# Host-side layouts in place of on-chip transposes, GpSimd pow for one norm, and an early weight load in an 8-core hybrid decoder trunk

## The chip, the cores and the metric

The kernel is one launch on all 8 cores of a Trainium2 chip (two dies, cores 0 to 3 and 4 to 7). No core talks to another: each does one prompt sequence and one share of the samples with the same weights. The metric is the device time of the slowest core in microseconds.

A program on all eight cores has two states here. In the fast one all cores agree within some 1%. In the slow one the cores of one die, sometimes of both, show a lower granted TensorE clock and the run takes some 2 to 14 per cent longer. Every comparison below is of fast runs, or of the cores of an undisturbed die, unless it says otherwise. The experiments ran on several chips; the fast runs of before beside them took 4237 to 4245 us, and one 4263, so a difference of a few us between two of them means little.

## The reference, cut to what matters

```
h = x                                           # (rows, 1024); 2048 prompt rows and 128 sample rows per core
for each of 4 layers:
    z = rmsnorm(h, g_mix) @ w_in                # columns: group A, then u, v (group B), then c_in (group C)
    A: y_a = gate_b * dwconv3(gate_c * xa)      # history hist_a: 2 rows per sample
    B: y_b = gelu(u) * (W_s @ layernorm(gelu(v)) + b_s)       # causal within chunks of 128 rows
    C: y_c = silu(layernorm(dwconv31(glu(c_in))))             # history hist_c: 30 rows per sample
    h += concat(rmsnorm(y_a), rmsnorm(y_b), rmsnorm(y_c)) @ w_out
    h += (silu(f @ w_gate) * (f @ w_up)) @ w_down             # f = rmsnorm(h)
    h += sigmoid(rmsnorm(h) @ w_ple_gate) * (p[i] @ w_ple_proj)
return rmsnorm(h), the new conv histories, the new v rows
```

Matrices are bf16 on the engine, x, p, the histories and all outputs are f32 in memory.

Of the kernel before, what the change touches and what calls it, by code (L numbers as in the profile page):

```python
# [7 lines left out]
F32 = mybir.dt.float32  # L8
# [5 lines left out]
DEPTH = 4  # L14
# [13 lines left out]
NV = NVL * DEPTH + 8  # L28
ENGS = ("pe", "act", "dve", "pool", "sp")
# [57 lines left out]
def build_program():  # L87
# [8 lines left out]
    xin = din("xin", [2176, D])  # L96
    pin = din("pin", [DEPTH, 2176, 256])
    sa = din("sa", [DEPTH, 32, 384])
    sc = din("sc", [DEPTH, 480, 256])
# [14 lines left out]
    y_o = dout("y", [2176, D])  # L114
    nap_o = dout("nap", [DEPTH, 2, 384])
    nas_o = dout("nas", [DEPTH, 32, 384])
    ncp_o = dout("ncp", [DEPTH, 30, 256])
    ncs_o = dout("ncs", [DEPTH, 480, 256])
# [5 lines left out]
    with es:  # L124
# [18 lines left out]
        STG = sb("STG", [128, 2, 1024], F32)  # L143
# [15 lines left out]
        NEGH = sb("NEGH", [128, 1], F32)  # L159
        PSTG = sb("PSTG", [128, 4, 256], F32)  # L160
# [5 lines left out]
        semnames = list(ENGS) + [f"d{i}" for i in range(NDS)] + [f"w{i}" for i in range(NS)]  # L166
        SEM = {n: es.enter_context(nc.semaphore("s_" + n)) for n in semnames}

        st = {"bank": 0, "sbank": 0, "ds": 0, "stg": 0, "sq": 0, "rb": 0, "tmp": 0, "pstg": 0, "pumpk": 3}
# [216 lines left out]
        def transpose_in(src_rows_ap, nrows, ncolchunks, evac):  # L386
            pass

# [3 lines left out]

        for hf in range(2):
# [18 lines left out]
            for (col0, row0, _) in tiles:  # L412
                si = ring("stg", 2)
                bi = blk_of_col(col0)
                for hh_ in range(2):
                    dma(STG[:, si, hh_ * 512:(hh_ + 1) * 512], xin[row0:row0 + 128, hh_ * 512:(hh_ + 1) * 512],
                        writes=[("STG", si, hh_)], fence=[("STG", si)])
                for half8 in range(2):
                    bank = newbank()
                    for k4 in range(4):  # L420
                        kc = half8 * 4 + k4
                        S.op("pe", lambda e, kc=kc, k4=k4, bank=bank, si=si: e.transpose(
                            PS[:, bank, k4 * 128:(k4 + 1) * 128], STG[:, si, kc * 128:(kc + 1) * 128], IDF[:]),
                            reads=[("STG", si, half8), ("STG", si), ("IDF",)], writes=[("ps", bank)], inc=(1 if k4 == 3 else 0))
                    S.op("act" if half8 == 0 else "dve",
                         (lambda e, bank=bank, half8=half8, col0=col0: e.activation(
                             H[:, half8 * 4:half8 * 4 + 4, col0:col0 + 128],
                             PS[:, bank, :].rearrange("p (k c) -> p k c", k=4), AF.Copy)) if half8 == 0 else
                         (lambda e, bank=bank, half8=half8, col0=col0: e.tensor_copy(
                             H[:, half8 * 4:half8 * 4 + 4, col0:col0 + 128],  # L430
                             PS[:, bank, :].rearrange("p (k c) -> p k c", k=4))),
                         writes=[("ps", bank)] + [("H", half8 * 4 + k, bi) for k in range(4)])

            for l in range(DEPTH):
# [15 lines left out]
                if hf == 0:  # L450
                    for j in range(2):
                        S.op("pool", lambda e, j=j: e.memset(GB[:, j, 0:30], 0.0), writes=[("Gh", j)])
                    si = ring("stg", 2)
                    dma(STG[0:32, si, 0:384], sa[l], writes=[("STG", si)])
                    bank = newbank()
                    for j in range(3):
                        S.op("pe", lambda e, j=j, bank=bank, si=si: e.transpose(
                            PS[:, bank, j * 32:(j + 1) * 32], STG[0:32, si, j * 128:(j + 1) * 128], IDF[0:32, 0:32]),
                            reads=[("STG", si), ("IDF",)], writes=[("ps", bank)], inc=(1 if j == 2 else 0))
                    S.op("dve", lambda e, bank=bank: e.tensor_copy(  # L460
                        XAH[:, :, :], PS[:, bank, 0:96].rearrange("p (j c) -> p j c", j=3)),
                        writes=[("ps", bank), ("XAH",)])
                    for rt in range(4):
                        nr = 128 if rt < 3 else 96
                        si = ring("stg", 2)
                        dma(STG[0:nr, si, 0:256], sc[l, rt * 128:rt * 128 + nr, :], writes=[("STG", si)])
                        bank = newbank()
                        for j in range(2):
                            S.op("pe", lambda e, j=j, bank=bank, si=si, nr=nr: e.transpose(
                                PS[:, bank, j * 128:j * 128 + nr], STG[0:nr, si, j * 128:(j + 1) * 128],  # L470
                                IDF[0:nr, 0:nr]),
                                reads=[("STG", si), ("IDF",)], writes=[("ps", bank)], inc=(1 if j == 1 else 0))
                        S.op("dve", lambda e, bank=bank, rt=rt, nr=nr: e.tensor_copy(
                            GFS[:, :, rt * 128:rt * 128 + nr],
                            PS[:, bank, 0:256].rearrange("p (j c) -> p j c", j=2)[:, :, 0:nr]),
                            writes=[("ps", bank)] + [("GFS", j) for j in range(2)])
                    for j in range(2):
                        S.op("pool", lambda e, j=j: e.tensor_copy(GB[:, j, GS0:GS0 + 480], GFS[:, j, 0:480]),
                             reads=[("GFS", j)], writes=[("Gsh", j)])
                else:  # L480
                    for j in range(2):
                        S.op("pool", lambda e, l=l, j=j: e.tensor_copy(GB[:, j, 0:30], CARG[:, l, j, :]),
                             reads=[("CARG", l)], writes=[("Gh", j)])

                pt_h = {}
                pload, ptrans = [], []
                for ti_, (col0, row0, _) in enumerate(tiles):
                    pi = ti_ % 4

                    def pld(pi=pi, row0=row0, l=l):  # L490
                        dma(PSTG[:, pi, :], pin[l, row0:row0 + 128, :], writes=[("PSTG", pi)])
                    pload.append(pld)

                    def pstep(pi=pi, col0=col0):
                        bank = newbank()
                        for j in range(2):
                            S.op("pe", lambda e, j=j, bank=bank, pi=pi: e.transpose(
                                PS[:, bank, j * 128:(j + 1) * 128], PSTG[:, pi, j * 128:(j + 1) * 128], IDF[:]),
                                reads=[("PSTG", pi), ("IDF",)], writes=[("ps", bank)], inc=(1 if j == 1 else 0))
                        S.op("act", lambda e, bank=bank, col0=col0: e.activation(  # L500
                            PT[:, :, col0:col0 + 128], PS[:, bank, 0:256].rearrange("p (j c) -> p j c", j=2), AF.Copy),
                            writes=[("ps", bank), ("PT", col0 // 128)])
                    ptrans.append(pstep)
                for ti_ in range(min(4, ntile)):
                    bg_add([pload[ti_]])
                for ti_ in range(ntile):
                    pt_h[ti_] = bg_add([ptrans[ti_]])
                    if ti_ + 4 < ntile:
                        bg_add([pload[ti_ + 4]])
# [27 lines left out]
                for tbi, tb in enumerate(range(0, ntile, 3)):  # L537
                    batch = list(range(tb, min(tb + 3, ntile)))
                    for ti_ in batch:
# [13 lines left out]
                             writes=[("BST", gi)])  # L553
                        pump(st["pumpk"])
                    if tbi + 1 < nblk:
                        u_block(tbi + 1)
                    for ti_ in batch:
                        col0, row0, kind = tiles[ti_]
                        gi = ti_ % 3
                        S.op("act", lambda e, gi=gi: e.activation(BST[:, gi, 7:8], BST[:, gi, 7:8], AF.Ln, bias=EPSC[:, 0:1]),  # L560
                             reads=[("EPSC",)], writes=[("BST", gi)])
                        S.op("act", lambda e, gi=gi: e.activation(BST[:, gi, 7:8], BST[:, gi, 7:8], AF.Exp, scale=-0.5),
                             writes=[("BST", gi)])
# [46 lines left out]
                if hf == 0:  # L610
# [3 lines left out]
                    for rt in range(4):  # L614
                        nr = 128 if rt < 3 else 96
                        bank = newbank()
                        for j in range(2):
                            S.op("pe", lambda e, j=j, bank=bank, rt=rt, nr=nr: e.transpose(
                                PS[0:nr, bank, j * 128:(j + 1) * 128],
# [455 lines left out]
```

## The kernel before: what the change and the argument touch

On the chip everything lies transposed: features on the 128 partitions, tokens along the free axis. Memory has tokens as rows, so the kernel before turns every input and output block with a TensorE transpose against an identity (IDF), by way of PSUM and a staging buffer. A core works through its tokens in two halves. The first half has blocks of 512, 512 and 128 columns (the last are the samples), the second 384, 384 and 256; each half runs all four layers. In a layer the order is: U and V (group B's two inputs), group C's two inputs, conv C by diagonal matrices DG, W_s, group A, w_out, the SwiGLU pair, and P, the gated p stage, which ends the layer.

Loading x, one 128-row tile at a time through two STG buffers (S.op puts an operation into an engine's queue; reads, writes and fences give the waits):

```python
for (col0, row0, _) in tiles:
    si = ring("stg", 2)
    for hh_ in range(2):
        dma(STG[:, si, hh_*512:(hh_+1)*512], xin[row0:row0+128, hh_*512:(hh_+1)*512], ...)   # SyncE's queue
    for half8 in range(2):
        bank = newbank()
        for k4 in range(4):
            S.op("pe", transpose(PS[:, bank, k4*128:(k4+1)*128], STG[:, si, kc*128:(kc+1)*128], IDF))
        S.op("act" if half8 == 0 else "dve", copy(H[:, half8*4:half8*4+4, col0:col0+128], PS[:, bank, :]))
```

The histories and the state outputs go the same way through the same two STG buffers, p through four PSTG buffers with its copies on ScalarE, y through STG again. (cut)

The layer norm of V, a batch of three 128-row tiles at a time (in short form):

```python
for ti_ in batch:                                # V matmuls, Gelu into one of three VG buffers, statistics
    mmgroup(PS[:, bk, 0:384], ...); S.op("act", VG[gi] = Gelu(PS[bk]))
    S.op("dve", bn_stats); S.op("dve", bn_aggr)
if tbi + 1 < nblk: u_block(tbi + 1)              # the next block of U: matmuls and three Gelus
for ti_ in batch:
    S.op("act", BST = Ln(var + EPS)); S.op("act", BST = Exp(-0.5 * BST))
    S.op("dve", VG = (VG - mean) * rstd)
    S.op("pool", VG = VG * gain); S.op("pool", VN = VG + bias)
```

Weights come through a ring of five slots by GpSimd's DMA queue; `try_load()` fills the slots that are free, and before it is first called when the first matmul group is built. W_s is loaded into VG and masked into MP by GpSimd, so the first V Gelu of a layer has to wait for MP.

## Time and profile before

| kernel before, five runs | us |
|---|---|
| median | 4734.76 |
| the one fast run (the profiled one) | 4257.77 |
| the four slow runs | 4687.31 to 4795.66 |

In profile lines PE is TensorE, PEld its weight loads, ACT ScalarE, DVE VectorE, POOL GpSimd and SP SyncE; a "q" behind the name marks the engine's instruction queue, where DMAs are issued. L310 is line 310 of the kernel that ran, PS is PSUM (where matmuls write), SLOT a weight slot. A DMA has landed when its data is in place. Read the profile in this order: the cores (is the run fast?), the busy shares (PE is highest), the slices (where does PE dip?), then what ends the waits in the dips. The lines stand in the prediction below.

### The profile page before, as it was taken

To read this page: it belongs to the slowest core of one execution; us is meant where nothing else is said; L and a number is where in the kernel's file an instruction comes from. 1 tells how busy PE (TensorE), PEld (TensorE's weight loads), DVE (VectorE), ACT (ScalarE), POOL (GpSimd) and SP (SyncE) were. 2 spreads that over 40 slices of the span, in tenths; PEclk is the share of its full clock that TensorE was granted. 3 is DMA by queue.
4 is the path that set the end of the run, shared out by engine and by line. 5 is a ranking of instruction groups with operands and counts; after the bars stand their busy time and mean duration, and the time that the engine had idled before them with its cause. 6 is when DMAs were issued, how large, how long until landed. Compare 5 with 4: busy or idle time off the path is not lost.

```text
span 4256.2 us, 67802 instructions; the slowest of 8 cores (4208.0 to 4256.2 us)
## 1 busy us (share of the span) xinstructions
PE 3737.4 (88%) x23068; PEld 2146.4 (50%) x23068; DVE 1861.0 (44%) x3543; ACT 1427.8 (34%) x2817; POOL 514.7 (12%) x642
## 2 busy tenths in 40 slices
PE   6899979799887999779996789987998789987997
PEld 3444534355443554435543556654665556654665
DVE  3452263622545325453253452455326353455325
ACT  3331143511435214342144341254215341344214
POOL 2100013000030000300000200020001200020010
PEclk9988999899998999989996999998999899998998
DMA  5333444244351442513435335441445335441542
GB/s 107 50 53 52 64 60 56 40 66 63 50 74 29 66 72 44 80 17 60 70 53 130 45 57 80 70 62 37 75 65 73 45 58 79 70 62 23 76 74 64
DMA packets 363568, 263.00 MB, mean 62 GB/s; under 512 B 117076, under 2 KB 330084, under 8 KB 363236
## 3 DMA queue, kind: packets, MB, share of 16 engines
q0 software_dynamic: 333696, 216.03, 36.8%
q1 hardware_dynamic: 29540, 42.65, 3.2%
q8 instruction: 196, 3.21, 0.3%
q14 instruction: 136, 1.11, 0.1%
HBM read 461.86 MB, written 12.78 MB: 112 GB/s over the span
## 4 chain that ended last, share of the span: by engine, by line
PE 69%; DVE 9%; ACT 8%; DMA 6%; issue 5%; POOL 1%; DVEq 0%; SPq 0%; ACTq 0%; POOLq 0%
PE PS L310 65%; DVE NRM L373 4%; PE PS L362 3%; DMA SLOT<-w_down 2%; DMA SLOT<-w_ple_gate 1%; DVE TMP L750 1%; ACT L316 1%; ACT L699 1%; ACT L560 1%; POOL VG L567 1%; DVE XA L735 1%; DMA STG<-xin 1%; ACT SQ L354 1%; ACT RB L316 1%; POOL VN L577 1%
## 5 line engine op out<-in xcount | busy, mean ns | idle before, releaser
L310 PE MATMUL PS<-NRM,SLOT 128*128 128x512 bf16 (+3 forms) x14592 | 2434.9, 326 | 96.1 <-DVE NRM L373 18.9
L310 PEld LDWEIGHTS PS<-NRM,SLOT 128*128 128x128 bf16 x14592 | 1359.8, 100 | 1088.2 <-issue 264.9
L883 ACT ACTIVATE TMP<-PS 128x512 f32<-128x512 f32 (+3 forms) x528 | 249.3, 473 | 1453.4 <-PE PS L310 1411.1
L885 DVE TENSOR_TENSOR Y<-TMP,PS 128x512 bf16<-128x512 f32 (+3 forms) x528 | 281.0, 532 | 1004.5 <-PE PS L310 879.5
L310 PE MATMUL PS<-Y,SLOT 128*128 128x512 bf16 (+3 forms) x4224 | 670.7, 319 | 12.5 <-DMA SLOT<-w_down 12.2
L310 PEld LDWEIGHTS PS<-Y,SLOT 128*128 128x128 bf16 x4224 | 385.4, 98 | 289.6 <-issue 41.1
L901 DVE TENSOR_TENSOR H<-H,PS 128x512 f32<-128x512 f32 (+3 forms) x576 | 300.2, 531 | 355.4 <-PE PS L310 338.5
L362 PE MATMUL PS<-SQ,ONES 128*128 128x512 bf16 (+3 forms) x816 | 213.8, 345 | 131.5 <-ACT SQ L354 128.3
L354 ACT ACTIVATE SQ<-H 128x512 bf16<-128x512 f32 (+3 forms) x624 | 274.5, 496 | 158.5 <-PE PS L362 101.9
L373 DVE SCALAR_TENSOR_TENSOR NRM<-H,VEC,RB 128x512 bf16<-128x512 f32 (+3 forms) x576 | 305.8, 603 | 42.6 <-ACT RB L318 42.2
L310 PE MATMUL PS<-GB,DG 128*128 128x512 bf16 (+3 forms) x1488 | 233.1, 317 | 0.0
L272 POOL DMA_DIRECT2D SLOT<-w_gate x72 | 63.6, 883 | 1132.8 <-PE PS L310 603.4
L362 PEld LDWEIGHTS PS<-SQ,ONES 128*128 128x128 bf16 x816 | 79.6, 101 | 228.7 <-issue 188.6
L310 PEld LDWEIGHTS PS<-GB,DG 128*128 128x128 bf16 x1488 | 134.7, 97 | 96.7 <-issue 1.7
L272 POOL DMA_DIRECT2D SLOT<-w_up x72 | 63.3, 879 | 838.8 <-PE PS L310 796.9
L932 DVE TENSOR_TENSOR TMP<-TMP,PS 128x512 f32<-128x512 f32 (+3 forms) x192 | 101.3, 528 | 119.8 <-ACT TMP L930 110.8
L316 ACT ACTIVATE RB<-PS,EPSC 128x512 f32<-128x512 f32 (+3 forms) x150 | 84.5, 563 | 167.3 <-PE PS L362 149.3
L272 POOL DMA_DIRECT2D SLOT<-w_in x104 | 92.0, 906 | 342.6 <-PE PS L362 204.1
L854 DVE TENSOR_TENSOR H<-H,PS 128x512 f32<-128x512 f32 (+3 forms) x192 | 97.5, 528 | 80.3 <-PE PS L310 65.8
L930 ACT ACTIVATE TMP<-PS 128x512 f32<-128x512 f32 (+3 forms) x192 | 86.9, 471 | 135.5 <-PE PS L310 80.5
L310 PE MATMUL PS<-PT,SLOT 128*128 128x512 bf16 (+3 forms) x384 | 92.3, 323 | 41.5 <-DVE TMP L932 33.0
L735 DVE TENSOR_TENSOR XA<-TMP,PS 128x512 f32<-128x512 f32 (+3 forms) x72 | 38.1, 530 | 176.7 <-PE PS L310 86.6
(113 smaller groups left out, 2322.9 us busy)
## 6 DMA issues: line engine op xcount, KB each, us to landing
SLOT<-w_gate POOLq DMA_DIRECT2D x48, 768.0 KB, 7.3
SLOT<-w_up POOLq DMA_DIRECT2D x48, 768.0 KB, 10.1
SLOT<-w_down POOLq DMA_DIRECT2D x48, 768.0 KB, 8.0
SLOT<-w_in POOLq DMA_DIRECT2D x72, 256.0 KB, 9.2
SLOT<-w_in POOLq DMA_DIRECT2D x16, 768.0 KB, 11.3
SLOT<-w_out POOLq DMA_DIRECT2D x16, 768.0 KB, 15.5
SLOT<-w_ple_gate POOLq DMA_DIRECT2D x16, 768.0 KB, 7.3
STG<-xin SPq DMA_DIRECT2D x34, 256.0 KB
```

The costliest lines, as they stand in the source:

```text
L272: S.op("pool", lambda e, dst=dst, src=src: e.dma_start(out=dst, in_=src), writes=[("slot", si)], sem=f"w{si}", inc=16, serialize=(pi_ == 0))
L310: S.op("pe", lambda e, l_=l_, r_=r_, i=i: e.matmul(out_ap, l_, r_, start=(i == 0), stop=(i == n - 1)), reads=rk, writes=[("ps", bank)], in ...
L316: S.op("act", lambda e: e.activation(rb, PS[:, bank, 0:n], AF.Ln, bias=EPSC[:, 0:1], scale=inv_n), reads=[("EPSC",)], writes=[("ps", bank) ...
L354: S.op("act", lambda e: e.activation(sq, src[:, c, c0:c0 + n], AF.Square), reads=[(srckey, c, bi)] + list(extra_reads), writes=[("SQ", qi)])
L362: S.op("pe", lambda e: e.matmul(PS[:, bank, 0:n], ONES[:], sqj, start=(k == 0), stop=(k == nchk - 1)), reads=[("SQ", qj), ("ONES",)], writ ...
L373: S.op("dve", lambda e, c=c: e.scalar_tensor_tensor(dst[:, c, c0:c0 + n], src[:, c, c0:c0 + n], gcol(c), rb, ALU.mult, ALU.mult), reads=[( ...
L854: S.op("dve", lambda e, bk=bk, m=m, c0=c0, n=n: e.tensor_tensor(H[:, m, c0:c0 + n], H[:, m, c0:c0 + n], PS[:, bk, 0:n], ALU.add), writes=[ ...
L883: S.op("act", lambda e, bg_=bg_, tmp=tmp, n=n: e.activation(tmp, PS[:, bg_, 0:n], AF.Silu), writes=[("ps", bg_), ("TMP", ti)])
L885: S.op("dve", lambda e, bu=bu, tmp=tmp, jl=jl, c0=c0, n=n: e.tensor_tensor(ACTB[:, jl, c0:c0 + n], tmp, PS[:, bu, 0:n], ALU.mult), reads=[ ...
L901: S.op("dve", lambda e, bk=bk, m=m, c0=c0, n=n: e.tensor_tensor(H[:, m, c0:c0 + n], H[:, m, c0:c0 + n], PS[:, bk, 0:n], ALU.add), writes=[ ...
L930: S.op("act", lambda e, bg_=bg_, tmp=tmp, n=n: e.activation(tmp, PS[:, bg_, 0:n], AF.Sigmoid), writes=[("ps", bg_), ("TMP", ti)])
L932: S.op("dve", lambda e, bp=bp, tmp=tmp, n=n: e.tensor_tensor(tmp, tmp, PS[:, bp, 0:n], ALU.mult), writes=[("ps", bp), ("TMP", ti)])
```

## The change

Its intent is to take everything off TensorE that isn't the model's own arithmetic: the host transposes x, p and the histories on the way in and y and the new histories on the way out, and DMA writes straight to the place of use. With the staging buffers gone, two copies per tile on ScalarE and VectorE go too. V's rstd leaves ScalarE, and the first weights are asked for at once.

```diff
+        try_load()                                   # ahead of the loop over the halves
-            (x by rows through STG, 136 transposes, copies on ScalarE and VectorE)
+            xv = xin.rearrange("(kc p) t -> p kc t", p=128)
+            for bi, (c0, n, kind) in enumerate(blocks):
+                for half8 in range(2):
+                    dma(H[:, k0:k0 + 4, c0:c0 + n], xv[:, k0:k0 + 4, r0:r0 + n], ...)
-                    (both histories by rows through STG, transposes, copies on VectorE)
+                    dma(XAH[:], sa[l].rearrange("(j p) c -> p j c", p=128), ...)
+                    dma(GFS[:, :, 0:480], sc[l].rearrange("(j p) c -> p j c", p=128), ...)
-                (p by rows through PSTG, 136 transposes in the background, copies on ScalarE)
+                    S.op("pool", dma_start(out=PT[:, :, c0:c0 + n], in_=pv[:, :, r0:r0 + n]))   # casts to bf16
+                        S.op("dve", BST = BST + EPS)                       # per tile
-                        S.op("act", BST = Ln(BST + EPS)); S.op("act", BST = Exp(-0.5 * BST))
+                    S.op("pool", BST[:, 0:nb_, 7:8] = BST[:, 0:nb_, 7:8] pow NEGH)   # per batch of three
-                    (conv C and conv A state outputs: transposes, copies on VectorE, STG, DMA)
+                    dma(ncs_o[l]..., GFS[:, :, 128:608]); dma(ncp_o[l]..., GFT); dma(nas_o..., XA...); dma(nap_o..., XA...)
-            (y: 136 transposes, copies, STG, DMA by rows)
+            for bi ...: dma(yv[:, k0:k0 + 4, r0:r0 + n], Y[:, k0:k0 + 4, c0:c0 + n], ...)
```

(Cut to its core; host and declarations follow suit.)

## The prediction

> **What bounds the kernel now.** First the cores: one execution of before is known in its state, the profiled one, 4257.77 us, all eight cores within 4208.0 to 4256.2 us at granted clocks near 0.93. The other four runs took 4687.31 to 4795.66 us; being over 1.5% above the fastest they count as slow. So the median, 4734.76 us, is a slow-state number. I work in the fast state and come back to this.
>
> The page of the slowest core comes next:
>
> ```profile
> PE 3737.4 (88%) x23068; PEld 2146.4 (50%) x23068; DVE 1861.0 (44%) x3543; ACT 1427.8 (34%) x2817; POOL 514.7 (12%) x642
> PE   6899979799887999779996789987998789987997
> PE 69%; DVE 9%; ACT 8%; DMA 6%; issue 5%; POOL 1%; DVEq 0%; SPq 0%; ACTq 0%; POOLq 0%
> ```
>
> PE sets the time. It is 90% busy or more in much of the 40 slices and dips at the two ends, in the middle (the hand-over between the two token halves) and at layer starts. Any gain must come from PE's own work or from those dips. The page's groups, and the same list by shape, give the pieces that the change touches:
>
> ```profile
> L422 PE MATMUL PS<-IDF,STG 128*128 128x128 f32 x136 | 33.3, 425 | 29.8 <-DMA STG<-xin 24.4 <-POOL DM L303 5.3
> L497 PE MATMUL PS<-IDF,PSTG 128*128 128x128 f32 x136 | 26.1, 313 | 9.2 <-DMA PSTG<-pin 8.0 <-ACT BST L560 0.6 <-DVE GFS L473 0.6
> L958 PE MATMUL PS<-IDF,Y 128*128 128x128 f32 x136 | 25.4, 358 | 8.2 <-ACT STG L962 5.8 <-DVE STG L965 2.5
> L560 ACT ACT_TABLE_LOAD x22 | 28.2, 1283 | 1.4 <-DVE BST L552 1.1
> L548 ACT ACT_TABLE_LOAD x24 | 30.8, 1283 | 36.4 <-POOL VN L577 34.1 <-PE PS L310 2.2
> ```
>
> The three big transposes are 85 us of PE, under 2.5% of the span; what surrounds them is larger. That is in the chain in order of time: the start of a later layer of the first half, the hand-over, and the end (start us, us, what).
>
> ```profile
> 48.76 10.58 DMA SLOT<-w_in
> ...
> 623.92 6.07 DVE NRM L373 x7
> 629.99 0.21 DVE TMP L932
> 630.20 0.14 issue
> 630.33 0.68 PE PS L469 x2
> 631.13 7.20 DMA STG<-sc
> ...
> 2257.52 2.78 DMA y<-STG
> 2261.93 2.73 DMA y<-STG
> ...
> 2276.71 3.60 DMA STG<-xin
> ...
> 4238.64 4.26 DMA y<-STG
> ```
>
> To see: the first weight load is issued only at 48.76 us; layer 1 waits 7.20 us for a conv history that is staged through two buffers; in the hand-over stores and loads take turns through the same two buffers. In the timeline, the first projection matmul starts at 59.58 us (U, then V: group B's two inputs; P is the stage that ends a layer), and in the hand-over none runs between 2244.4 and 2316.66 us.
>
> **What the Trainium skill says.** "ScalarE: Activation LUTs", section "What ACT_TABLE_LOAD costs": about 1283 ns each time ScalarE changes its set of functions. The trace agrees: 1283 ns for each of the 22 loads before the layer norm's Ln. "DMA: Bandwidth & Descriptors", section "SWDGE vs HWDGE vs iDMA": a DMA that casts has to be issued from GpSimd. So the new f32-to-bf16 loads of p join the weight loads in GpSimd's queue; the same page, "Issuing engines are not separate DMA queues", says that all issuers share 16 engines. Here the trace shows 36.8% of them for the weight queue, 3.2% for the other. "TensorE: Matmul & The Clock Gate", "Part 4: PE-mode transpose", gives about 275 to 390 ns for a bf16 128x128 transpose and an eviction after it; here f32 ones read 313 to 425 ns.
>
> **The change, part by part.** The host now transposes x, p, the two states and all outputs but the v rows; DMA writes them straight to or from their place. PE loses all f32 transposes, ACT and DVE their evictions. Layer norm B's rstd becomes one DVE add per tile and one GpSimd pow per three tiles. Five weight slots are filled before anything else. The large matmuls keep count and order.
>
> Start. DMA rates, as estimates from the page: 42.65 MB in 3.2% of 4256 us is 313 GB/s when busy; the weight queue's 216.03 MB in 36.8% is 138 GB/s of bf16 written. Block 0 of x is 2.1 MB; sharing evenly with weights issued at about 5 us it needs some 13 us, so it lands near 15 us, the first weights by about 17. Add four remaining squares (4 x 0.53), 2.9 us from last square to rstd, 0.8 to the first normalised chunk: first matmul at about 21 us instead of 59.6. **38 us.**
>
> Starts of layers 1 to 3, first half. With no transposes in PE's queue, the first U group can start at 623.4 us; the second needs a PSUM bank that DVE frees at 630.2 (its eight norm multiplies come first). Before, the second ran at about 643. The wait of 7.20 us is 5.8 and 5.5 us in the other layers. I take 11 us each: **33 us.**
>
> V stage. Before, Ln sits in ACT's queue behind the next U block's three Gelus and costs a table load there and one back. In layer 1 PE idles 4.29 us until a Gelu and 1.56 until DVE's product after a late Sigmoid; in the second half 2.40 and 2.60 us. After, add and pow start when the last tile's statistics are there, while PE does the U block, about 5.7 us. No pow was run here; I guess 1 us for three columns, from 1060 ns of GpSimd's 384-column product. Saved 5 us a layer in the first half (2 in layer 0, where the W_s tile now lands behind x), 4.5 in the second (3 in its first layer): 3x5+2+3x4.5+3 = **33.5 us.**
>
> The p transposes: eight or nine pairs at 0.22 us in the chain, 2 us in each of the six layers that do not stand at a start: **12 us.**
>
> State outputs. Conv C history: PE idle 1.40 and 0.36 us and 1.5 us of transposes in the first half, 3.3 a layer; 2.0 in the second: **21 us.** Conv A: PE waited 13.0 and 14.3 us in all for DVE XA, with 24 transposes at 0.3; most of 35, say **29 us.**
>
> Hand-over. The last norm multiply stays near 2256.8 us. Then the x loads go out, behind about 1.7 us of remaining stores; 1.57 MB for block 0 at 313 GB/s is 5 us, 2 more to land: 2266. Norm again 5.5: first matmul at 2271.5 instead of 2316.66. **45 us.**
>
> End. Last multiply at 4237.0, then one 0.5 MB store of about 4.3 us: 4241.5 instead of 4256.2. **14.5 us.**
>
> Sum: 38+33+33.5+12+21+29+45+14.5 = 226 us, 4257.8 to 4032. I take 5% of the gain back, since PE gets denser: the granted clock was 0.91 in the dense stretch 124 to 612 us, 0.93 over all. That makes **4045 us**, 5% less.
>
> **The rivals.**
> 1. Only the 85 us of transposes count and the gaps return as other waits (DVE's norm multiplies, PSUM banks). For: DVE already ends PE waits at layer starts. Against: the chain runs through the loads themselves. It gives 4258 - 85, about 4170 us.
> 2. GpSimd becomes the bound of the V stage: pow, two 2.5 us casts of the history, three more DMA issues and two products per tile stand in one queue. For: it was busy 26.5 of 54.6 us in layer 1's stage (639.64 to 694.19). Against: the casts no longer wait for the history. A pow of 5 us instead of 1 would cost some 4 us x 24 batches: about 4140 us.
> 3. The start is hidden or bound by bandwidth: x, five slots and constants are some 12 MB at about 280 GB/s, 43 us, so early matmuls could wait for weights; and W_s behind x holds the first Gelu of V, as it uses its buffer. That would give back 10 to 20 us: about 4060.
> 4. The denser PE lowers the die's clock by 1%: about 35 us, 4080.
>
> **Range and chances.** In the fast state I expect 3995 to 4095 us: rival 1 or 2 in part makes the upper end, bubbles of cold clock that vanish too make the lower. But the printed median of before is slow, four runs in five, near 4760. If after's median is slow too, the same microseconds off give about 4530. I can't foresee the state, so the range runs to 4550. Fast against fast, faster by over 2% needs 85 us out of 225: 0.95; within 2% 0.04; slower 0.01.
>
> **What would show it.** First projection matmul near 21 us and near 2271 us; U starting right after the P matmuls in layers 1 to 3, then a wait for DVE TMP; no ACT table load between Gelus of V except for a norm's Ln; conv31 directly after the C matmuls; a tail under 6 us after the last norm multiply. I am wrong if GpSimd's pow takes over 2 us, if V's Gelus still wait for POOL VN, if x lands after 25 us, or if the dense stretch's clock falls below 0.90.

## The result, and the profile after

| | changed, us | before, us | ratio |
|---|---|---|---|
| first series: median of all runs | 4157.53 (9 runs) | 4533.03 (16 runs) | |
| first series: fast runs | 4054.41 to 4095.22 | from 4257.77 | 0.9542 (0.9501 to 0.9583) |
| again, on the chip of the first experiments: fast runs | 4061.94, 4063.49, 4064.29 | 4239.77 to 4263.10 | 0.9570 (0.9538 to 0.9602) |

A ratio is the mean time of one kernel's fast runs over that of the other's fast runs of the same rounds, with a 95% interval, so it isn't quite the ratio of medians. The changed kernel is faster by 4.3 to 4.6 per cent. Below, "the changed kernel" is 4063.2 us, the mean of its three fast runs of the second series.

The first profile of the changed kernel fell into the slow state (granted clocks 0.913 to 0.922); the one of the second series is fast. Its page has these lines for busy shares, PE's slices, the granted clock and the chain:

```profile
PE 3601.4 (89%) x22357; PEld 2057.4 (51%) x22552; DVE 1824.3 (45%) x3513; ACT 1312.4 (32%) x2543; POOL 547.4 (13%) x690
PE   6799987999888998889986799887998799987997
PEclk9899998999999999989997899998999899998999
PE 72%; DVE 9%; ACT 8%; issue 4%; DMA 4%; POOL 2%; SPq 1%; DVEq 0%; ACTq 0%; another core or an unknown queue 0%; POOLq 0%
```

PE's busy time fell by 136 us (3737.4 to 3601.4), but 195 matmul records are missing here (22357 against 22552 weight loads); at 0.32 us each, the mean of the page's largest group, they would be some 60 us (an estimate), and what is left is near the 85 us of the transposes. The share of DMA in the chain fell from 6 per cent (5 in before's second profile) to 4. The dips at the start, the middle and the end are still there, narrower.

For an account I took a second fast-state profile of before too (experiment e9) and read both timelines on core 0, whose spans are 4219.5 and 4052.5 us. Stage limits are matmuls that both kernels have: the first of U, the first and last with DG, the first of W_s and of the down-projection, the last of P. Changes are summed over the eight layers of both halves (us); some 11 us between the down-projection and P, the same in both, are in no row:

| piece | before | changed | saved | forecast |
|---|---|---|---|---|
| start, to the first U matmul | 60.2 | 26.6 | 33.7 | 38 |
| layers 1 to 3, first half: from the last P to the first DG matmul (start, U, V, C's inputs) | 209.1 | 159.7 | 49.4 | 33 + part of V, p, conv C |
| same stretch, layers 1 to 3, second half | 160.6 | 144.3 | 16.3 | part of V, p, conv C |
| U, V, C's inputs in layer 0 of both halves | 132.6 | 123.9 | 8.7 | part of V, conv C |
| conv C | 331.2 | 319.0 | 12.2 | part of conv C |
| end of conv C to the first down-projection matmul (W_s, group A, w_out, a third of gate and up) | 1284.4 | 1281.6 | 2.8 | 29 |
| down-projection with the rest of gate and up | 1519.2 | 1527.1 | -7.9 | 0 |
| P | 403.4 | 407.1 | -3.7 | 0 |
| hand-over, last P to first U | 76.1 | 35.4 | 40.8 | 45 |
| end, from the last P | 32.0 | 17.0 | 15.0 | 14.5 |
| sum (the spans differ by 167.0) | | | 167 | 226 |

Three places in the timeline show what changed. First a layer's start (layer 1, first half). The columns are start, length, engine, line, operation, output and inputs, shape, count, and in brackets the idle time ahead of it with what ended it. Before, second profile, core 0:

```profile
594.01 0.28 PE L310 MATMUL PS<-PT,SLOT 128*128 128x128 bf16 x2
...
601.21 1.09 PE L469 MATMUL PS<-IDF,STG 128*128 128x128 f32 x4 [6.62 <-DVE TMP L932]
607.83 1.24 PE L469 MATMUL PS<-IDF,STG 128*128 128x128 f32 x4 [5.54 <-DMA STG<-sc]
609.29 4.89 PE L310 MATMUL PS<-NRM,SLOT 128*128 128x512 bf16 x15 [0.22 <-DVE GFS L473]
```

Changed, core 0:

```profile
562.28 0.28 PE L310 MATMUL PS<-PT,SLOT 128*128 128x128 bf16 x2
562.55 3.13 PE L310 MATMUL PS<-NRM,SLOT 128*128 128x512 bf16 x8
569.48 3.57 PE L310 MATMUL PS<-NRM,SLOT 128*128 128x512 bf16 x8 [3.79 <-DVE TMP L850]
```

U follows P at once, and the second group waits for VectorE's TMP, as predicted. Now group A. Both kernels have the same squares for a norm there; before, one of the state transposes follows:

```profile
1308.53 0.53 PE L362 MATMUL PS<-SQ,ONES 128*128 128x512 bf16 x1 [4.19 <-ACT SQ L354]
1311.02 0.37 PE L765 MATMUL PS<-IDF,XA 128*32 128x128 f32 x1 [1.97 <-DVE XA L735]
1311.18 2.34 PE L310 MATMUL PS<-NRM,SLOT 128*128 128x512 bf16 x5
```

Changed, the same place:

```profile
1242.97 0.58 PE L362 MATMUL PS<-SQ,ONES 128*128 128x512 bf16 x1 [4.19 <-ACT SQ L354]
1243.95 4.04 PE L310 MATMUL PS<-NRM,SLOT 128*128 128x512 bf16 x8 [0.39 <-DVE NRM L373]
```

The transpose and its wait of 1.97 us are gone, and the matmul begins 0.98 instead of 2.65 us after the start of the last square. But it needs normalised chunks, which VectorE makes one by one: eight matmuls now take 4.04 us, at 505 ns each, where five took 2.34 (468 ns). The waits for XA (13.1 and 14.3 us in the list of waits of before) stood in the shadow of the norm. Over all eight layers the stretch gave 2.8 us; no run undid A's outputs alone.

The hand-over. SyncE's queue in the changed kernel, core 0, then PE:

```profile
2110.76 28.12 SPq L217 DMA_DIRECT2D y<-Y  x6
2139.03 16.89 SPq L217 DMA_DIRECT2D H<-xin  x6
2156.02 2.11 SPq L217 DMA_DIRECT2D LNB<-lnb  x1
2158.22 0.38 SPq L217 DMA_DIRECT2D VG<-wsT  x1
```

```profile
2154.12 1.72 PE L362 MATMUL PS<-SQ,ONES 128*128 128x384 bf16 x4 [20.30 <-ACT SQ L354]
2161.25 4.18 PE L310 MATMUL PS<-NRM,SLOT 128*128 128x384 bf16 x8 [2.16 <-DVE NRM L373]
```

x's loads stand behind all six y stores. A store takes 0.37 to 0.38 us to issue; for the rest of the 28.12 us the queue waits for y itself, VectorE's last norm, whose multiplies end at 2138.37. The loads go out at 2139.03 and let the squares run at 2154.12: 15 us from the first issue to the first matmul over squares. I had guessed 5 us of transfer and 2 of landing.

### The profile page after: what moved, and what is told of

It is laid out like the page before. It is cut to its first block, busy times and chain, and to the rows that moved or that the text cites. A ratio compares the mean times of both kernels' runs of the same rounds, so it can differ in the third digit from the quotient of the medians.

```text
span 4155.9 us, 65608 instructions; the slowest of 8 cores (4122.0 to 4155.9 us)
## 1 busy us (share of the span) xinstructions
PE 3735.2 (90%) x22552; PEld 2093.6 (50%) x22552; DVE 1826.8 (44%) x3513; ACT 1314.2 (32%) x2543; POOL 547.2 (13%) x690
## 4 chain that ended last, share of the span: by engine, by line
PE 75%; DVE 8%; ACT 6%; DMA 4%; issue 4%; POOL 1%; DVEq 0%; ACTq 0%; SPq 0%; POOLq 0%
PE PS L310 72%; DVE NRM L373 4%; PE PS L362 3%; DMA SLOT<-w_down 1%; DMA SLOT<-w_ple_gate 1%; ACT L316 1%; DMA H<-xin 1%; ACT L629 1%; ACT RB L316 1%; POOL VG L514 1%; DVE Y L373 1%; DVE TMP L850 1%; POOL VN L524 1%; DVE TMP L680 1%; ACT L638 0%
## 5 line engine op out<-in xcount | busy, mean ns | idle before, releaser
L310 PE MATMUL PS<-NRM,SLOT 128*128 128x512 bf16 (+3 forms) x14592 | 2503.6, 332 | 114.1 <-DVE NRM L373 25.3
L310 PEld LDWEIGHTS PS<-NRM,SLOT 128*128 128x128 bf16 x14592 | 1375.0, 101 | 1163.2 <-issue 477.5
L310 PE MATMUL PS<-Y,SLOT 128*128 128x512 bf16 (+3 forms) x4224 | 680.9, 322 | 6.6 <-DMA SLOT<-w_down 6.4
L310 PE MATMUL PS<-GB,DG 128*128 128x512 bf16 (+3 forms) x1488 | 244.6, 328 | 1.0 <-DVE GFT L548 0.8
```

Source lines behind the costliest of these rows:

```text
L310: S.op("pe", lambda e, l_=l_, r_=r_, i=i: e.matmul(out_ap, l_, r_, start=(i == 0), stop=(i == n - 1)), reads=rk, writes=[("ps", bank)], in ...
```

## The experiments

Line numbers of the experiments' kernels shift by a few. e2_pow_alone was a first build of the kernel with pow alone; it didn't fit into SBUF and never ran. e5_pow_alone2 is the same with a smaller constant.

**e1_changed_again: the changed kernel again.** No edit.

> The changed kernel as it is, for a profile in the fast state and more fast runs beside before. Theory A (the forecast's sum, fast against fast, is right; only the number on the record line was set against a printed median that is mostly slow runs): 0.950 to 0.958 of before, fast against fast, and the profile shows the first projection matmul near 26.6 us as in the changed kernel's first trace. Rival B (the gain is only what PE lost in transposes, the rest is a matter of which state a run fell in): a ratio of 0.975 to 0.98 in fast runs.

Measured: 4061.94, 4063.49 and 4064.29 us fast, ratio 0.9570 (0.9538 to 0.9602), as theory A has it and far from rival B's 0.975; the profile is the one read above.

**e3_no_pow: the changed kernel with Ln and Exp on ScalarE again.**

```diff
-    S.op("dve", BST = BST + EPS)
-    S.op("pool", BST = BST pow NEGH)                 # per batch
+    S.op("act", BST = Ln(BST + EPS)); S.op("act", BST = Exp(-0.5 * BST))   # per tile
```

> The changed kernel with Ln and Exp on ACT again, all else kept. Theory A: about 33 us slower than the changed kernel, ratio to before 0.962. Rival (with the transposes gone the V stage has room and the pow is worth little): 10 us or less, ratio 0.956.

Measured: one fast run, 4069.57 us, 6 us more than the changed kernel. The dies' median spans in the two profiles (4048.4 and 4049.8 us against 4056.3 and 4059.8) say 8 to 10. Within the changed kernel pow is worth some 6 to 10 us. By stage (core 5 in both) the stretches from the last P to the first DG matmul grew by 14 us; the down-projection and P, which the edit doesn't touch, were 6 us shorter.

**e5_pow_alone2: the kernel before with pow alone.**

```diff
+    S.op("dve", BST = BST + EPS)
+    S.op("pool", BST = BST pow NEGH)                 # per batch
-    S.op("act", BST = Ln(BST + EPS)); S.op("act", BST = Exp(-0.5 * BST))
```

> The kernel before, with layer norm B's rstd by one VectorE add per tile and one GpSimd pow per batch instead of ScalarE's Ln and Exp; all transposes stay. Theory of the record: the wait for the norm in V is ScalarE's queue and its table loads, 33.5 us, which is there with the transposes too: 4243 (before in the earlier rounds, fast) to about 4210. Rival, after the run that put Ln and Exp back into the changed kernel cost only some 8 us: the norm's time lies mostly beside the U products, and the 33.5 was over-counted; then 5 to 12 us less, about 4235. A third way: pow is slower where DVE is loaded with transposes; then no gain.

Measured: 4207.82 to 4214.88 us in six fast runs, against 4237.34 to 4240.03 of before: ratio 0.9934 (0.9916 to 0.9952), 28 us; by stage (core 5 against e9's core 0) 24 of them lie between the last P and the first DG matmul. So the same edit is worth 28 us beside the transposes and 6 to 10 without them. The timeline of layer 1 in the second half suggests why. ScalarE in before (second profile, core 0), U starting at 2770.47:

```profile
2791.11 0.39 ACT L500 ACTIVATE PT<-PS 128x256 bf16<-128x256 f32 x1 [0.88 <-PE PS L497]
2791.51 1.28 ACT L560 ACT_TABLE_LOAD   x1
...
2797.84 0.49 ACT L548 ACTIVATE VG<-PS 128x384 f32<-128x384 f32 x1
```

ScalarE in e3, the changed kernel with Ln and Exp (core 5), U starting at 2651.16:

```profile
2669.41 1.28 ACT L505 ACT_TABLE_LOAD   x1
...
2675.87 0.49 ACT L493 ACTIVATE VG<-PS 128x384 f32<-128x384 f32 x1
```

GpSimd in the changed kernel (core 5), U starting at 2642.11:

```profile
2663.37 0.89 POOL L505 TENSOR_TENSOR BST<-BST,NEGH 128x3 f32<-128x3 f32 x1 [12.69 <-DVE BST L499]
2664.99 1.10 POOL L514 TENSOR_TENSOR VG<-VG,LNB 128x384 f32<-128x384 f32 x1 [0.73 <-DVE VG L511]
2666.23 0.99 POOL L524 TENSOR_TENSOR VN<-VG,LNB 128x384 bf16<-128x384 f32 x1
...
2673.34 0.86 POOL L505 TENSOR_TENSOR BST<-BST,NEGH 128x3 f32<-128x3 f32 x1 [1.93 <-DVE BST L499]
```

The Ln's table load comes 21.0 us after U's first matmul in before, behind p's copies in ScalarE's queue, and 18.3 us after it in e3, where those copies are gone. In e3 it is over before VectorE has the third tile's statistics (bn_aggr, which makes the mean and variance, starts at 2671.54), so this load costs nothing there; only the one back to Gelu does, 1.28 us. The first Gelu of V's second batch, which frees PSUM for PE, comes after 27.4 us in before, 24.7 in e3 and, with pow, at 2667.31, 25.2 us after U. After that a batch takes 10.0 us with pow (2663.37 to 2673.34) and 10.7 with Ln (2669.41 to 2680.12): six GpSimd products of about 1 us fill most of either. My reading: the V stage had one slack to give; taking p's copies out of ScalarE's queue gives most of it, taking Ln and Exp out does too, and the forecast booked it once for each. This is argued from one layer's timeline; no run took p's copies alone out of before. What is shown is that PE's waits for V's Gelu are not gone. From the lists of PE's waits on core 0 (us in total, times, longest), before and changed:

```profile
PE PS L310 <- ACT VG L548: 16.9, 6, 4.3
PE PS L310 <- ACT VG L493: 17.6, 24, 1.7
```

With pow alone it was 9.3 us. And the Gelu waits for GpSimd's product VN, which frees its buffer: 54.0 us in all before, 100.0 us in the changed kernel.

**e4_x_old: the changed kernel with x by rows and transposed on TensorE.** 
```diff
-    dma(H[:, k0:k0 + 4, c0:c0 + n], xv[:, k0:k0 + 4, r0:r0 + n])          # per block and half
+    dma(STG[:, si, ...], xin[row0:row0 + 128, ...])                       # per tile, two buffers
+    4 x S.op("pe", transpose(PS, STG, IDF)); S.op("act" or "dve", copy(H, PS))
```

> The changed kernel with x again loaded row by row and transposed on PE, at the start and in the hand-over; outputs, states, p, pow and the early weights as changed. Theory A: start 10 to 15 us later than the changed kernel's 26.6 us (the p and state loads stay out of the way and the weights stay early), hand-over 25 us longer, together 35 to 40 us, ratio 0.963. Rival (direct x loads are bound by bandwidth and buy nothing): within 10 us of the changed kernel.

Measured: 4103.27, 4110.10, 4108.64 us fast, ratio 0.9679 (0.9636 to 0.9722): 44 us lost. The first U matmul is at 56.1 us (core 5), the hand-over's gap 52.9 us.

**e6_p_old: the changed kernel with p by rows and transposed.**

```diff
-    S.op("pool", dma_start(out=PT[:, :, c0:c0+n], in_=pv[:, :, r0:r0+n]))
+    dma(PSTG[:, pi, :], pin[l, row0:row0+128, :])            # SyncE's queue, four buffers
+    2 x S.op("pe", transpose(PS[...], PSTG[:, pi, ...], IDF)); S.op("act", copy(PT[:, :, col0:col0+128], PS[...]))
```

> The changed kernel with p loaded by rows and transposed on TensorE, in the way of before (its evictions on ScalarE); the rest as changed. Theory of the record: 12 us on the path, so 4064 goes to about 4076. Rival A: all 26 us of transposes and the waits for the bank count, since PE is busy around 90 per cent: 4090 to 4100. Rival B: p's transposes fill PE's idle stretches at the starts and behind the norms and cost nothing: 4064.

Measured: one fast run, 4123.52 us; the undisturbed die of the profile has a median span of 4109.1 against 4049 of the changed kernel. 60 us lost, more than any theory said. On core 5 layers 1 to 3 take 518.9 us in the first half as in the changed kernel (519.0 to 521.8), so in the middle of the run p's transposes are free. The loss is in the start (first U matmul at 64.1 us) and the hand-over (gap 59.9 us). SyncE's queue at the start, and PE:

```profile
30.13 21.78 SPq L218 DMA_DIRECT2D PSTG<-pin  x9
```

```profile
42.33 0.66 PE L461 MATMUL PS<-IDF,PSTG 128*128 128x128 f32 x2 [42.33 <-DMA PSTG<-pin]
```

p's loads go out behind x and the constants, and p's transposes stand ahead of x's norm in PE's queue, so PE's very first instruction waits 42 us for data that nothing needs before P.

**e7_states_in_old: the changed kernel with both histories by rows, through STG, and transposed.** 
```diff
-    dma(XAH[:], sa[l]...); dma(GFS[:, :, 0:480], sc[l]...)
+    dma(STG[0:32, si, 0:384], sa[l]); 3 x transpose; S.op("dve", copy(XAH, PS))
+    for rt in range(4): dma(STG[0:nr, si, 0:256], sc[l, rows]); 2 x transpose; S.op("dve", copy(GFS, PS))
```

> The changed kernel with the two convolution histories of the sample rows loaded by rows through a two-deep staging buffer and transposed on TensorE; the rest as changed. Theory of the record: the starts of the layers of the first half wait for the load again; 3 layers of 11 us, 33 us more, 4064 to 4097. Rival A: what stood in the way was the load together with p's and x's transposes in one queue; alone the history's load is early enough, and 0 to 10 us are lost. In the trace the wait for DMA STG<-sc at the start of layer 1 (7.20 us before) tells which.

Measured: 4122.11 and 4122.45 us fast, ratio 0.9725 (0.9697 to 0.9753): 59 us lost. The waits at the layers' starts are back (7.09 us for DMA STG<-sc in layer 1, gaps of 16.1, 15.2 and 14.0 us on core 5), of which the rest of each layer gives back 4 to 8 us: 8, 9 and 10 us net, 27 of the forecast 33. (This profile is of a slow run; core 5 too lost clock, 0.932 in the mean, but only in the last layer, behind the stretches read here.) The other half is the start: the first U matmul at 58.4 us, behind the histories' transposes.

**e8_states_out_old: the changed kernel with the state outputs by transposes and copies.** 
```diff
-    dma(ncs_o[l]..., GFS[:, :, 128:608]); dma(ncp_o[l]..., GFT); dma(nas_o..., XA...); dma(nap_o..., XA...)
+    per piece: S.op("pe", transpose(PS, GFS or GFT or XA, IDF)); S.op("dve", copy(STG, PS)); dma(out rows, STG)
```

> The changed kernel with the four state outputs (both convolutions, prompt and sample rows) made by transposes on TensorE, copies on VectorE and a staging buffer; the rest as changed. Theory of the record: 21 us for convolution C and 29 us for convolution A, 50 us more, 4064 to 4114. Rival A: PE's waits for DVE XA are not the transposes' but those of the convolution itself, and come back in another place: only C's 21 and the transposes' own 10 us count, about 4090. Rival B: nothing but the transposes' own time, some 20 us.

Measured: 4088.49 and 4090.17 us fast, ratio 0.9647 (0.9619 to 0.9675): 26 us lost, near rival A. By stage (core 5 against core 0 of e1), conv C and the stretch ahead of it (where C's transposes stand) grow by 11.8 and 17.7 us, and the stretch that holds group A's transposes by 2.7; the down stage is 10 us shorter in this profile. Conv C's outputs were worth about what I had booked, group A's almost nothing; the two are told apart by stage alone.

**e9_before_again: the kernel before, for a second profile.** No edit.

> The kernel before, unchanged, for a second profile of it in the fast state: the first one was taken at 4258, while the fast runs beside the experiments so far read 4237 to 4243. Expected: 4240 if the profile falls in the fast state; the time from the first U matmul of layer 0 to its last P matmul, 560 us on one core of the first profile at a clock of 0.81 in part of it, becomes 530 to 540 as in the kernel with pow alone. If it stays at 560, pow's 28 us lie in layer 0.

Measured: 4267.72 us, fast by its clocks (0.923 to 0.940), and layer 0 takes 534.1 us on core 0. The 560 us on one core of the first profile came with a clock of 0.80 in part of it (from 168 to 353 us); this is not the transposes' work. On core 0 (span 4219.5) the pieces can be compared.

**e10_y_old: the changed kernel with y transposed and staged.** 
```diff
-    dma(yv[:, k0:k0 + 4, r0:r0 + n], Y[:, k0:k0 + 4, c0:c0 + n])          # per block and half
+    8 x S.op("pe", transpose(PS, Y[:, kc, col0:col0 + 128], IDF)); S.op("act" / "dve", copy(STG, PS))
+    dma(y_o[row0:row0 + 128, :], STG[:, si_, :])                          # per tile, two buffers
```

> The changed kernel with y transposed on TensorE, evicted by ScalarE and VectorE through the two-deep staging buffer and stored by rows; the rest as changed. Theory of the record: the end grows by 14.5 us, and the hand-over by what of its 45 us is not x's (the run with x by rows showed 18 us there): some 20 us more, about 4098. Rival: the transposes fill PE's idle time while x loads, so the hand-over stays at 35 us and only the end counts: about 4078.

Measured: 4081.84 and 4085.97 us fast, ratio 0.9630 (0.9602 to 0.9658): 21 us lost, between the two. The hand-over's gap grows by 10 us (45.4 against 35.4, core 0) and the end from 17.0 to 33.3 us (core 5).

**e11_no_early: the changed kernel without the early filling of the weight slots.**

```diff
-        try_load()                                   # ahead of the loop over the halves
```

> The changed kernel without the early filling of the weight slots: the first weights are asked for when the first group is built, behind the histories and p. Theory of the record: the start's 38 us need both x's direct load and the early weights; without them the first U matmul moves from 27 us to 40 to 50 us, 4064 to about 4082. Rival: weights asked for late still land by about 30 us, since GpSimd has nothing ahead of them but constants; below 5 us lost.

Measured: one fast run, 4073.07 us, 10 us lost. The first U matmul moves from 27.0 to 44.2 us (core 2), waiting 26.58 us for the first weights. On this core the layer gives 7 us back, mostly in the down stage (206.7 to 201.4 us), on core 0 nothing; what the early fill is worth lies between 10 and 17 us of the start's 38.

**e12_both_ahead: two orders altered.**

```diff
+        try_load()                                   # now ahead of GpSimd's constants
         dma(VEC[:], vec, ...)
@@ end of the first half
-            for bi ...: store y block bi             # all six stores, then the next half's x
+            for bi ...: load x block bi of the next half; store y block bi
```

> The changed kernel with two orders altered: the first five weight loads are issued ahead of GpSimd's constants (one constant took 4.29 us there beside VectorE's work, and the first weights left only at 9.42 us), and in the hand-over each block of the next half's x is asked for before the y store of the same place, not behind all of them. Theory of the reading: both gaps are queue order, so the first U matmul comes at about 21 us (27 before) and the hand-over's gap falls from 35 to about 16 us: 4064 to about 4040. Rival: the hand-over is bound by bandwidth (its window showed the DMA engines full), so x takes the stores' place and only some 5 us are won there; and the start is bound by x's own landing at 14 us and the norm: then about 4055.

Measured: 4053.73 to 4057.38 us in five of six fast runs (the sixth 4081.86), ratio 0.9575 (0.9534 to 0.9616). Without the sixth that is 8 us faster than the changed kernel's 4063.2, near the rival's number; but the ratio is no better than its 0.9570, and in the first series the changed kernel itself had runs of 4054.41 and 4056.17, so whole runs don't show a gain. The stages do (core 1), and not for the rival's reason. Both gaps did shrink as the theory said, from 27 to 22 us and from 35 to 17. U, V and C's inputs of those layers grew by 6 and 10 us. The hand-over on core 5, SyncE's queue first, then GpSimd, then PE:

```profile
2137.30 9.29 SPq L217 DMA_DIRECT2D y<-Y  x2
...
2148.94 0.65 SPq L217 DMA_DIRECT2D VG<-wsT  x1
```

```profile
2160.70 0.86 POOL L430 TENSOR_SCALAR_AFFINE_SELECT MP<-VG 128x768 bf16<-128x768 f32 x1 [35.36 <-DMA VG<-wsT]
```

```profile
2166.91 0.37 PE L363 MATMUL PS<-SQ,ONES 128*128 128x256 bf16 x1 [15.79 <-ACT SQ L355]
```

W_s is asked for at 2148.94, behind the last y stores, MP comes at 2160.70, V's first Gelu after that, and the squares for the next norm stand behind this Gelu in ScalarE's queue: PE waits 15.79 us, 2.53 in the changed kernel.

**e13_order: and W_s early.**

```diff
             load x block 0
+            load W_s, WSA, LNB, BSP, BSS of layer 0          # start: behind x block 0
             load x blocks 1, 2
@@ hand-over: x0, y0, x1, then
+            load W_s, WSA, LNB, BSP, BSS of layer 0
             load x block 2, store y block 1, store y block 2
```

> The kernel with both orders altered (weights ahead of GpSimd's constants; each block of the next half's x ahead of the y stores), with one order more: in SyncE's queue the token-mixing weights of layer 0 (W_s, its biases and norm constants) go out right behind the first block of x at the start, and behind the second block of x in the hand-over, where the last two y stores now come last. Reading of the run with both orders: it brought the first U matmul forward by 5 us at the start and 18 us in the hand-over, but U and V of these two layers grew by 6 and 10 us, since V's first Gelu waited 5.72 and 10.79 us for GpSimd's MP, which W_s feeds and whose buffer the Gelu uses, and the squares for the next norm stood behind it. Theory: with W_s early the Gelus no longer wait, U and V of the second half's first layer fall from 70 to about 58 us and those at the start from 70 to about 61: 4055 to about 4036. Rival: the DMA engines are full there, so early W_s delays x's later blocks or the stores by as much, and the squares wait for x itself: no gain, 4050 to 4058.

Measured: the two fast runs are 4042.83 and 4046.38 us, beside 4244.94 and 4245.03 of before in the same rounds (4044.6 / 4245.0 = 0.953; too few runs for an interval). Against the changed kernel's 4063.2 that is 19 us less, and both runs are below the fastest of any series of it, 4054.41: as far as two runs can show it, it beats both kernels. The undisturbed die of its profile shows where, core 0:

```profile
2123.73 0.51 SPq L217 DMA_DIRECT2D VG<-wsT  x1
...
2136.41 12.34 SPq L217 DMA_DIRECT2D y<-Y  x4
```

```profile
2151.78 0.27 PE L363 MATMUL PS<-SQ,ONES 128*128 128x256 bf16 x1 [2.53 <-ACT SQ L355]
```

In the hand-over the theory holds: gap 17.4 us, U and V and C's inputs 61.0 us in all (69.6 in e12 on core 1; 59.5 in the changed kernel), the wait back to 2.53. At the start the rival holds: U begins at 21.6 us, but the stretch up to the first DG matmul grew to 72.4 us (64.3), so nothing is won there. What bounds the start now is not settled: a wait of 3.54 us for the squares of x's second block points to x's landing (that block's second part landed at 36.08), and x's last four loads take SyncE until 25.1 us to issue, but no run took bytes away to show it.

## Why the prediction was right or wrong

**Two things failed.** One is the figure, the other the size of a few terms of the sum; the mechanism of the rest held.

**The figure.** The step is "That makes **4045 us**, 5% less", held against the printed 4734.76. 4045 was worked out in the fast state, from 4257.8; the printed median is a slow one, as the text itself says, and the same microseconds off it "give about 4530". Set side by side the two figures read as 14.6 per cent. Measured were 4.3 to 4.6 per cent, fast against fast, where the working had 5.0; the changed kernel's 4063.2 lies inside the fast-state range of 3995 to 4095. The new median, 4157.53, mixes both states and lies inside the range for this reason alone. A forecast has to name its state in its figure, or take the printed one's.

**The sum.** 226 us were forecast and 13 of them taken back (5 per cent would be 11); 167 were found on core 0, and 178 between the typical fast runs (4241 and 4063). The steps that failed are the terms for conv A's outputs (29 us, measured 2.8), for the V stage and p (45.5 us together, measured 28 for pow alone beside the transposes, 6 to 10 without them, and 0 for p in the middle of the run) and the transfer time in the hand-over (7 us, measured 15). By its terms:

- *Start, 38:* 33.7. First matmul at 26.6, not 21. x's first block landed at 13.93 us, near the forecast 15 (its last at 31.93), but the weights left GpSimd only at 9.41 us, because its constant DM (an affine_select of 128 columns) took 4.29 us beside VectorE's build of DG, which also took 4.29; in before the same instruction took 0.34. They landed 16.9 us later, at 26.32, and PE waited 9.53 us for them; I had counted 12. e12 moved the weights ahead and the first matmul came at 22 to 23. On core 5, asking 7.9 us earlier made them land only 4.3 us earlier (27.22 to 22.89), while the second part of x's block 0 landed 3.9 us later (13.36 to 17.29): beyond queue order the start is shared transfer, which is rival 3 in part.
- *Starts of layers 1 to 3, 33:* right. U follows P at once, then waits for TMP; e7 puts 27 of it back by undoing this part alone.
- *V stage, 33.5, and p, 12:* too large; booked twice in part, as I read it. Beside the transposes pow gives 28 (e5), without them 6 to 10 (e3); p's transposes in the middle of the run cost nothing (e6, where pow leaves no Ln behind them in ScalarE's queue). My duration of pow was right: 0.86 to 0.89 us for three columns against a guess of 1. And with Ln or pow, GpSimd's six products fill most of a batch's time, which is rival 2 in a milder form: of my own signs of being wrong, "if V's Gelus still wait for POOL VN" came true, 100.0 us of such waits where before had 54.0.
- *Conv C's outputs, 21:* right; e8 puts 23 us on them (its 26 less group A's 2.7), by stage up to 30.
- *Conv A's outputs, 29:* wrong, 2.8 (2.7 by e8). The step was "PE waited 13.0 and 14.3 us in all for DVE XA, with 24 transposes at 0.3; most of 35, say **29 us**". A wait's length is no saving: the next matmul needed normalised chunks that come hardly earlier.
- *Hand-over, 45:* 40.7. The step "1.57 MB for block 0 at 313 GB/s is 5 us, 2 more to land" was off; it took 15 us, with the DMA engines full (the windows view, which counts a packet whole where it starts, gives their share as 1.11 in the window from 2126 to 2161 us).
- *End, 14.5:* 15.0.
- *Not booked:* the gate, up and down stage took 7.9 us more in this profile, with waits for w_down at 10.9 us (5.8 before). In e12 on core 1 the same stage took 1518 us, as in before, so I don't call it a cost of the change; its cause stays open, as does that of P's 3.7.

**The rivals.** Rival 1 (85 us, about 4170) fell. Rival 3 was right in its first half, early matmuls that wait for weights: the 9.53 us above. Its second named a real danger, W_s behind x holding V's first Gelu, but in the changed kernel itself it didn't bite: the wait for the second norm's squares there is 2.53 us. It became the bound once x was brought forward, most of all in the hand-over, where I hadn't looked for it (15.79 us in e12, 7.8 at the start on core 1). Rival 4 fell: the mean granted clock rose from about 0.936 to 0.947, which fits that a gap that vanished had been at a low one (0.54 in before's stretch 594 to 610 us). The down-projection's stage of layer 3, first half, took 200.7 us in both e9 and e12, so its matmuls got no faster.

**Undone alone, the parts add up to more than the whole.** x 44, p 60, histories 59, state outputs 26, y 21, pow 6: 216 us, of 178 (the early weights, 10 by e11, are not in it). The start and the hand-over are the reason. x's tiles, p's tiles or the histories alone each keep the first U matmul at 56 to 64 us; a gap with three causes closes only when the last one goes, and each of them undone pays for the whole of it.

## What to carry to other kernels

When a part is removed, book what the next instruction still waits for, not the length of the wait that goes; two parts that end the same gap must be booked once. Transfers are ordered by the queue that issues them: in each stall ask which load the first starved engine needs, and move that one ahead of everything that is merely next. State the clock state of every number, the forecast's too.

## What the Trainium skill lacked or had wrong

- "SBUF — State Buffer", section "SBUF: two separate sides", says that a GpSimd op that reads SBUF and a VectorE op with two SBUF inputs exclude each other for a whole instruction. The trace agrees. The durations that the page gives are of a DMA's descriptors; here are some of GpSimd's own instructions: the affine_select of 128 columns took 4.29 us beside VectorE's DG build (two inputs, 4.29 us), and 0.34 us without it; three of GpSimd's 24 MS products took 4.27 us, each beside such a build, against a median of 0.45.
- "GPSIMD Engine Reference" has no cost for pow. Here a pow of 128 x 3 f32 took 0.86 to 0.89 us and of 128 x 2 some 0.71, which gives, as an estimate from the two, some 0.4 us a call and 0.15 us a column: one call per batch of three costs about half of three calls.
- "DMA: Bandwidth & Descriptors", section "Issuing engines are not separate DMA queues", calls the time to issue a DMA usually small beside the DMA itself; it has no figure for it and doesn't say that it grows. Here a y store took 0.37 to 0.38 us to issue, and the six x loads behind them, with the DMA engines full, 1.52 to 5.57 us each, 16.89 in all, against 11.6 to 16.2 us to landing. Nor does it say what order in one queue can cost: a load of W_s that stands behind others set V's start: asked for 11.5 us ahead of U's first matmul (e13) instead of 11.6 behind it (e12), the wait for the squares fell from 15.79 to 2.53 us.
- "TensorE: Matmul & The Clock Gate", Part 1, tells one to budget 13/16 of the clock for dense matmuls on all cores. In fast runs here stretches of 100 us were granted 1.00 with PE busy all of it, and the mean over the span was 0.947; in slow runs the cores of one die or both fell to means of 0.78 to 0.93. What decides between the two states the page doesn't tell, and no run here shows it.
